# RoPE on one core: 64 rows of x to a partition, tables spread by TensorE, products from staged x

## The chip, the core and the metric

One of the eight cores of a Trainium2 chip. The metric is the device time of one execution in microseconds (us), lower is better; a kernel's number is the median of several runs, with the lowest and highest behind it. A profile is of one execution and its times count from the start of the profiled span, which is some 1.9 us shorter than the time of that run.

## The reference

```python
# x: (8, 8, 1024, 64) float32; cos_cached, sin_cached: (1024, 32) float32
x_first, x_second = x[..., :32], x[..., 32:]
out_first  = x_first * cos_cached - x_second * sin_cached
out_second = x_first * sin_cached + x_second * cos_cached
out = concatenate([out_first, out_second], axis=-1)
```

Each element of x is multiplied by a sine and by a cosine, and one half row is combined with the other. 16.8 MB come in and 16.8 MB go out. The tables are 128 KB each and are used 64 times over.

## The kernel before

x is cut into 16 chunks of 128 partitions by 32 rows (8 KB to a partition). A partition's 32 rows repeat every 32 partitions, so the tables are loaded once to 32 partitions and copied to the other 96: into PSUM for VectorE's products, into SBUF for GpSimd's. VectorE makes nearly all products; the sums go to GpSimd, to TensorE (with ScalarE copying back) or stay on VectorE.

```python
R = 32; F = R * hd; T = R * half; Q = seq // R; reps = P // Q      # Q = 32, reps = 4
csp = pt.tile([P, T], fp32, name="csp")      # PSUM, 2 banks each
snp = pt.tile([P, T], fp32, name="snp")
acc = pa.tile([P, F], fp32, name="acc")      # PSUM, 4 banks
nc.sync.dma_start(out=sn[0:Q], in_=sin_cached.rearrange("(p n) j -> p (n j)", p=Q))
nc.scalar.dma_start(out=cs[0:Q], in_=cos_cached.rearrange("(p n) j -> p (n j)", p=Q))
# ... all loads of x are issued at once ...
for r in range(reps):
    nc.vector.tensor_copy(out=snp[r * Q:(r + 1) * Q], in_=sn[0:Q])
    nc.scalar.copy(out=csp[r * Q:(r + 1) * Q], in_=cs[0:Q])

def products(eng, c, s, ctab, stab):
    xr = rows(xt[c])
    eng.tensor_tensor(out=rows(s), in0=xr, in1=tab(stab), op=TT.mult)
    eng.tensor_tensor(out=xr, in0=xr, in1=tab(ctab), op=TT.mult)
# ... per chunk: products on VectorE, then sums on GpSimd / TensorE / VectorE, then the store;
#     chunks 1 and 6 are GpSimd's alone, chunk 15 VectorE's alone
```

## Time and profile before

| | before |
|---|---|
| time, median (three runs) | 86.01 us (85.86 to 86.02) |
| span of the profiled run | 84.16 us |
| tables landed (sine, cosine) | 3.81, 4.13 |
| first product on VectorE | 8.87 |
| VectorE idle between first product and its end | 2.80 us in all |
| VectorE's last instruction ends | 77.18 |
| last byte stored | 82.70 |

The page's shares, the slices, the stretches and the end of the timeline stand in the prediction below. VectorE's timeline at the start (start and duration in us, then what it waited for in brackets) shows the table copies, from the landing to the first product, and one short wait for x:

```profile
3.84 5.00 DVE L73 COPY snp<-sn 32x1024 f32<-32x1024 f32 x4 [3.84 <-DMA sn<-in_sin_cached_dram]
8.87 2.29 DVE L88 TENSOR_TENSOR vs<-x,snp 128x2048 f32<-128x2048 f32 x1
...
13.99 2.29 DVE L88 TENSOR_TENSOR vs<-x,snp 128x2048 f32<-128x2048 f32 x1 [0.44 <-DMA x<-in_x_dram]
```

TensorE's timeline of the same kernel: each group is one float32 matmul that the trace shows as two. The second starts 1.83 us after the first, the fourth 0.86 us after the third. I read this as half clock for the first two ("cold") and a clock that was released about 3.5 us after the first began. It is read from the pace alone: the page's row of granted clock has nines at that time.

```profile
13.65 2.04 PE L119 MATMUL acc<-x,plus 128*128 128x512 f32 x2 [13.65 <-DVE x L89]
15.48 1.83 PE L120 MATMUL acc<-vs,minus 128*128 128x512 f32 x2
17.15 1.02 PE L119 MATMUL acc<-x,plus 128*128 128x512 f32 x2
18.01 1.02 PE L120 MATMUL acc<-vs,plus 128*128 128x512 f32 x2
```

### The profile page before, as it was taken

Reading aid. Unit: us, or ns where it says so; the run is one execution under the profiler, and the core shown is the slowest. Engines: PE = TensorE matmul, PEld = TensorE weight load, DVE = VectorE, ACT = ScalarE, POOL = GpSimd, SP = SyncE. Lnnn points to the kernel's source line nnn. Section 1 sums busy time; section 2 is a strip of 40 time slices with the busy share of each in tenths; the row PEclk is TensorE's granted clock in tenths of the full one; section 3 lists DMA queues with packets and bytes.
Section 4 is the critical chain, followed back from the end, with each engine's and each line's share of the span. In section 5 each row is a group of like instructions: output and inputs, shape, how many; then the busy total and the mean of one; then the engine's idle time right before and its main releaser. Section 6 shows DMA issues by size and latency. Waiting matters only on the chain.

```text
span 84.2 us, 363 instructions
## 1 busy us (share of the span) xinstructions
PE 40.1 (48%) x80; PEld 15.7 (19%) x80; DVE 70.4 (84%) x34; ACT 15.7 (19%) x16; POOL 71.4 (85%) x38
## 2 busy tenths in 40 slices
PE   0000005994930896895949497794949600000000
PEld 0000002422400341423314051332414100000000
DVE  0199997999999999999999982999999999996000
ACT  4399000004040003104040402204040310000000
POOL 3199999999999999999999999999999999970000
PEclk9999999999999569999999999999999999555555
DMA  3899999999999999999999999999999999999991
GB/s 29 282 432 409 420 420 436 417 409 420 436 428 409 417 428 432 432 424 409 421 436 436 432 421 417 424 424 436 432 432 432 413 421 428 428 436 407 432 419 55
DMA packets 4736, 33.82 MB, mean 402 GB/s; under 512 B 448, under 2 KB 448, under 8 KB 768
## 3 DMA queue, kind: packets, MB, share of 16 engines
q1 hardware_dynamic: 3824, 27.40, 78.7%
q10 hardware_dynamic: 912, 6.42, 18.1%
HBM read 17.04 MB, written 16.78 MB: 402 GB/s over the span
## 4 chain that ended last, share of the span: by engine, by line
POOL 53%; DVE 23%; issue 9%; DMA 4%; DVEq 1%; POOLq 0%
POOL x L94 13%; POOL x L93 11%; DVE vs L88 11%; POOL x L89 11%; POOL gs L88 11%; DVE x L89 8%; POOL sn L77 4%; DMA sn<-in_sin_cached_dram 4%; POOL cs L77 3%; DVE acc L88 3%; DVE x L93 1%; DVEq L170 1%; POOLq L93 0%; POOLq L77 0%
## 5 line engine op out<-in xcount | busy, mean ns | idle before, releaser
L119 PE MATMUL acc<-x,plus 128*128 128x512 f32 x40 | 23.3, 666 | 26.4 <-DVE x L89 13.6
L89 DVE TENSOR_TENSOR x<-x,csp 128x2048 f32<-128x2048 f32 x14 | 32.0, 2287 | 0.6
L88 DVE TENSOR_TENSOR vs<-x,snp 128x2048 f32<-128x2048 f32 x13 | 29.7, 2282 | 2.2 <-POOL x L94 1.7
L122 ACT COPY x<-acc 128x1024 f32<-128x1024 f32 x10 | 10.1, 1012 | 49.2 <-PE acc L120 49.2
L94 POOL TENSOR_TENSOR x<-x,vs 128x1024 f32<-128x1024 f32 (+1 forms) x9 | 19.0, 2108 | 0.0
L93 POOL TENSOR_TENSOR x<-x,vs 128x1024 f32<-128x1024 f32 (+1 forms) x9 | 18.9, 2105 | 0.0
L119 PEld LDWEIGHTS acc<-x,plus 128*128 128x128 f32 x40 | 7.5, 208 | 39.4 <-issue 23.9
L120 PE MATMUL acc<-vs,minus 128*128 128x512 f32 x20 | 11.6, 666 | 0.0
L120 PE MATMUL acc<-vs,plus 128*128 128x512 f32 x20 | 10.2, 592 | 0.0
L89 POOL TENSOR_TENSOR x<-x,cs 128x2048 f32<-128x2048 f32 x2 | 9.1, 4546 | 0.2
L88 POOL TENSOR_TENSOR gs<-x,sn 128x2048 f32<-128x2048 f32 x2 | 9.1, 4542 | 0.1
L73 DVE COPY snp<-sn 32x1024 f32<-32x1024 f32 x4 | 4.9, 1223 | 3.9 <-DMA sn<-in_sin_cached_dram 3.8
L120 PEld LDWEIGHTS acc<-vs,minus 128*128 128x128 f32 x20 | 4.4, 219 | 5.9 <-issue 5.9
L77 POOL COPY sn<-sn 32x1024 f32<-32x1024 f32 x3 | 3.1, 1032 | 2.7 <-DMA sn<-in_sin_cached_dram 2.6
L93 POOL TENSOR_TENSOR x<-x,gs 128x1024 f32<-128x1024 f32 x2 | 4.7, 2362 | 0.2
L94 POOL TENSOR_TENSOR x<-x,gs 128x1024 f32<-128x1024 f32 x2 | 4.7, 2357 | 0.0
L120 PEld LDWEIGHTS acc<-vs,plus 128*128 128x128 f32 x20 | 3.8, 190 | 4.8 <-issue 4.8
L74 ACT COPY csp<-cs 32x1024 f32<-32x1024 f32 x4 | 4.0, 1008 | 1.5 <-DMA cs<-in_cos_cached_dram 1.4
L77 POOL COPY cs<-cs 32x1024 f32<-32x1024 f32 x3 | 3.1, 1033 | 0.1
L88 DVE TENSOR_TENSOR acc<-x,snp 128x2048 f32<-128x2048 f32 x1 | 2.3, 2297 | 0.0
L71 ACT ACT_TABLE_LOAD x1 | 1.3, 1283 | 1.2 <-PEq L159 1.2
L93 DVE TENSOR_TENSOR x<-x,acc 128x1024 f32<-128x1024 f32 x1 | 1.2, 1223 | 0.0
(8 smaller groups left out, 2.4 us busy)
## 6 DMA issues: line engine op xcount, KB each, us to landing
x<-in_x_dram SPq DMA_DIRECT2D x7, 2048.0 KB, 25.0
out_dram<-x SPq DMA_DIRECT2D x9, 1024.0 KB, 13.0
out_dram<-x ACTq DMA_DIRECT2D x6, 1024.0 KB, 9.0
x<-in_x_dram SPq DMA_DIRECT2D x2, 1024.0 KB, 6.3
out_dram<-x SPq DMA_DIRECT2D x2, 512.0 KB, 6.0
cs<-in_cos_cached_dram ACTq DMA_DIRECT2D x1, 128.0 KB, 3.4
sn<-in_sin_cached_dram SPq DMA_DIRECT2D x1, 128.0 KB, 3.1
```

What stands on the lines that cost most here:

```text
L71: nc.scalar.mul(minus, plus, -1.0)
L73: nc.vector.tensor_copy(out=snp[r * Q:(r + 1) * Q], in_=sn[0:Q])
L74: nc.scalar.copy(out=csp[r * Q:(r + 1) * Q], in_=cs[0:Q])
L77: nc.gpsimd.tensor_copy(out=t[r * Q:(r + 1) * Q], in_=t[0:Q])
L88: eng.tensor_tensor(out=rows(s), in0=xr, in1=tab(stab), op=TT.mult)
L89: eng.tensor_tensor(out=xr, in0=xr, in1=tab(ctab), op=TT.mult)
L93: eng.tensor_tensor(out=xr[:, :, 0], in0=xr[:, :, 0], in1=sr[:, :, 1], op=TT.subtract)
L94: eng.tensor_tensor(out=xr[:, :, 1], in0=xr[:, :, 1], in1=sr[:, :, 0], op=TT.add)
L119: nc.tensor.matmul(a[:, k], plus, xr[:, :, k], start=True, stop=False)
L120: nc.tensor.matmul(a[:, k], plus if k else minus, sr[:, :, 1 - k], start=False, stop=True)
L122: nc.scalar.copy(out=xr, in_=a.rearrange("p k n j -> p n k j"))
L170: with _tile.TileContext(nc) as tc:
```

## The change

It means to cut the number of DMA packets (DMA is busy from end to end) by giving a partition 64 rows, so 16 KB packets instead of 8 KB. With 64 rows the tables repeat every 16 partitions and are twice as large, and would take all the eight banks of PSUM that the kernel before divides between tables and sums; so they live in SBUF. Three things follow. TensorE spreads them from 16 partitions to 128 with a matrix of zeros and ones. The first unit's products read the tables from PSUM, where TensorE has put them, while ScalarE copies them to SBUF. From then on ScalarE copies ("stages") each chunk of x to PSUM, and VectorE multiplies the staged chunk by the SBUF table.

```diff
-    R = 32
+    R = 64
-    csp = pt.tile([P, T], fp32, name="csp")
-    snp = pt.tile([P, T], fp32, name="snp")
-    acc = pa.tile([P, F], fp32, name="acc")
+    st = [ps.tile([P, 3 * BK], fp32, name=f"st{i}") for i in range(2)]   # PSUM, 3 banks each
+    acc = ps.tile([P, 2 * BK], fp32, name="acc")                         # PSUM, 2 banks
...
-    for r in range(reps):                       # copies of the tables
-        nc.vector.tensor_copy(out=snp[r * Q:(r + 1) * Q], in_=sn[0:Q])
-        nc.scalar.copy(out=csp[r * Q:(r + 1) * Q], in_=cs[0:Q])
+    part_s = [st[0][:, 0:BK], st[0][:, BK:2 * BK], st[0][:, 2 * BK:], acc[:, :BK]]
+    part_c = [st[1][:, 0:BK], st[1][:, BK:2 * BK], st[1][:, 2 * BK:], acc[:, BK:]]
+    for i in range(4):
+        for t, part in ((sn, part_s), (cs, part_c)):
+            nc.tensor.matmul(part[i], sel, t[0:Q, i * BK:(i + 1) * BK], start=True, stop=True)
...
+    def stage(u, i, n0, n1):
+        nc.scalar.copy(out=st[i][:, :(n1 - n0) * hd], in_=xt[u][:, n0 * hd:n1 * hd])
+    def products(u, i, n0, n1, alone):
+        ...
+        mul(nc.vector, sr, pr, tab(sn, n0, n1))
+        mul(nc.vector, pr if alone else xr, pr, tab(cs, n0, n1))
...
+    for i in range(4):                          # unit 0, straight from the tables in PSUM
+        direct(i)
+        pool_sums(0, i * G, (i + 1) * G)
+    for t, part in ((sn, st[0]), (cs, st[1])):
+        nc.scalar.copy(out=t[:, 0:2 * BK], in_=part[:, 0:2 * BK])
+    ...                                         # and the four remaining parts, 512 each
...
+    cuts = ((0, 24), (24, 48), (48, 64))        # three chunks to a unit of 64 rows
+    ahead = {1: [(pe_back, 1, 0)], 7: [(pe_back, 3, 16)], 10: [(pe_back, 4, 16)]}
+    behind = { ... }                            # sums, copies back and stores, chunk by chunk
+    put(0); put(1)                              # put = stage the chunk
+    for c, (u, n0, n1) in enumerate(chunks):
+        products(u, c % 2, n0, n1, (u, n0) in alone)
+        for f, *args in ahead.get(c, ()): f(*args)
+        put(c + 2)
+        for f, *args in behind.get(c, ()): f(*args)
```

More of the change, by code (lines that the diff above doesn't have):

```diff
@@ L28 @@
     Q = seq // R
-    reps = P // Q
-    n_ch = (b * h * seq) // (R * P)
-    G = 512 // half
-    assert seq % R == 0 and P % Q == 0 and Q % 32 == 0
+    n_u = (b * h * seq) // (R * P)
+    BK = 512
+    G = BK // half
+    assert seq % R == 0 and P % Q == 0 and n_u == 8 and R == 4 * G
     xf = x.rearrange("b h s d -> (b h s d)").rearrange(
-        "(c p m) -> c p m", p=P, m=F)
+        "(u p m) -> u p m", p=P, m=F)
     of = out.rearrange("b h s d -> (b h s d)").rearrange(
-        "(c p m) -> c p m", p=P, m=F)
+        "(u p m) -> u p m", p=P, m=F)
     ctx.enter_context(tc.manual_schedule())
@@ L41 @@
     xp = ctx.enter_context(tc.tile_pool(name="xp", bufs=1))
-    tv = ctx.enter_context(tc.tile_pool(name="tv", bufs=6))
+    tv = ctx.enter_context(tc.tile_pool(name="tv", bufs=3))
     tg = ctx.enter_context(tc.tile_pool(name="tg", bufs=1))
-    pt = ctx.enter_context(
-        tc.tile_pool(name="pt", bufs=1, space=bass.MemoryType.PSUM))
-    pa = ctx.enter_context(
-        tc.tile_pool(name="pa", bufs=1, space=bass.MemoryType.PSUM))
+    ps = ctx.enter_context(
+        tc.tile_pool(name="ps", bufs=1, space=bass.MemoryType.PSUM))
     cs = const.tile([P, T], fp32, name="cs")
     sn = const.tile([P, T], fp32, name="sn")
+    sel = const.tile([Q, P], fp32, name="sel")
     plus = const.tile([P, P], fp32, name="plus")
     minus = const.tile([P, P], fp32, name="minus")
-    csp = pt.tile([P, T], fp32, name="csp")
-    snp = pt.tile([P, T], fp32, name="snp")
-    acc = pa.tile([P, F], fp32, name="acc")
-    nc.sync.dma_start(out=sn[0:Q], in_=sin_cached.rearrange("(p n) j -> p (n j)", p=Q))
-    nc.scalar.dma_start(out=cs[0:Q], in_=cos_cached.rearrange("(p n) j -> p (n j)", p=Q))
-    xt = []
-    for first, n in [(0, 1), (1, 1)] + [(c, 2) for c in range(2, n_ch, 2)]:
-        t = xp.tile([P, n, F], fp32, name=f"x{first}")
-        nc.sync.dma_start(out=t, in_=xf[first:first + n].rearrange("c p m -> p c m"))
-        xt += [t[:, i] for i in range(n)]
+    st = [ps.tile([P, 3 * BK], fp32, name=f"st{i}") for i in range(2)]
+    acc = ps.tile([P, 2 * BK], fp32, name="acc")
+    nc.sync.dma_start(out=sn[0:Q], in_=sin_cached.rearrange("(q n) j -> q (n j)", q=Q))
+    nc.scalar.dma_start(out=cs[0:Q], in_=cos_cached.rearrange("(q n) j -> q (n j)", q=Q))
+    xt = [xp.tile([P, F], fp32, name=f"x{u}") for u in range(n_u)]
+    for m0, m1 in ((0, F // 2), (F // 2, F)):
+        nc.sync.dma_start(out=xt[0][:, m0:m1], in_=xf[0][:, m0:m1])
+    for u in range(1, n_u):
+        nc.sync.dma_start(out=xt[u], in_=xf[u])
+    nc.gpsimd.memset(sel, 0.0)
+    s3 = sel.rearrange("q (r j) -> q r j", j=Q)
+    nc.gpsimd.affine_select(out=s3, in_=s3, compare_op=TT.not_equal, fill=1.0,
+                            base=0, pattern=[[0, P // Q], [-1, Q]], channel_multiplier=1)
     nc.gpsimd.memset(plus, 0.0)
@@ L71 @@
     nc.scalar.mul(minus, plus, -1.0)
-    for r in range(reps):
-        nc.vector.tensor_copy(out=snp[r * Q:(r + 1) * Q], in_=sn[0:Q])
-        nc.scalar.copy(out=csp[r * Q:(r + 1) * Q], in_=cs[0:Q])
-    for t in (sn, cs):
-        for r in range(1, reps):
-            nc.gpsimd.tensor_copy(out=t[r * Q:(r + 1) * Q], in_=t[0:Q])
-    def rows(t, n0=0, n1=R):
+    part_s = [st[0][:, 0:BK], st[0][:, BK:2 * BK], st[0][:, 2 * BK:], acc[:, :BK]]
+    part_c = [st[1][:, 0:BK], st[1][:, BK:2 * BK], st[1][:, 2 * BK:], acc[:, BK:]]
@@ L80, in rows, with tab @@
+    for i in range(4):
+        for t, part in ((sn, part_s), (cs, part_c)):
+            nc.tensor.matmul(part[i], sel, t[0:Q, i * BK:(i + 1) * BK], start=True, stop=True)
+    def rows(t, n0, n1):
         return t[:, n0 * hd:n1 * hd].rearrange("p (n k j) -> p n k j", k=2, j=half)
-    def tab(t, n0=0, n1=R):
+    def tab(t, n0, n1):
         v = t[:, n0 * half:n1 * half].rearrange("p (n o j) -> p n o j", o=1, j=half)
         return v.to_broadcast([P, n1 - n0, 2, half])
-    def products(eng, c, s, ctab, stab):
-        xr = rows(xt[c])
-        eng.tensor_tensor(out=rows(s), in0=xr, in1=tab(stab), op=TT.mult)
-        eng.tensor_tensor(out=xr, in0=xr, in1=tab(ctab), op=TT.mult)
@@ L91, in sums @@
-    def sums(eng, c, s, n0, n1):
-        xr, sr = rows(xt[c], n0, n1), rows(s, n0, n1)
-        eng.tensor_tensor(out=xr[:, :, 0], in0=xr[:, :, 0], in1=sr[:, :, 1], op=TT.subtract)
-        eng.tensor_tensor(out=xr[:, :, 1], in0=xr[:, :, 1], in1=sr[:, :, 0], op=TT.add)
-    def store(q, c, n0=0, n1=R):
-        q.dma_start(out=of[c][:, n0 * hd:n1 * hd], in_=xt[c][:, n0 * hd:n1 * hd])
-    def on_pool(c):
-        s = tg.tile([P, F], fp32, name="gs")
-        products(nc.gpsimd, c, s, cs, sn)
-        sums(nc.gpsimd, c, s, 0, R)
-        store(nc.sync, c)
@@ L105, in vector_pool @@
-    def vector_pool(c, cuts=(0, R)):
-        s = tv.tile([P, F], fp32, name="vs")
-        products(nc.vector, c, s, csp, snp)
-        for n0, n1 in zip(cuts, cuts[1:]):
-            sums(nc.gpsimd, c, s, n0, n1)
-            store(nc.sync, c, n0, n1)
-    def vector_tensor(c):
-        s = tv.tile([P, F], fp32, name="vs")
-        products(nc.vector, c, s, csp, snp)
-        for n0 in range(0, R, G):
-            xr, sr = rows(xt[c], n0, n0 + G), rows(s, n0, n0 + G)
-            a = acc[:, n0 * hd:(n0 + G) * hd].rearrange("p (k n j) -> p k n j", k=2, j=half)
-            for k in range(2):
-                nc.tensor.matmul(a[:, k], plus, xr[:, :, k], start=True, stop=False)
-                nc.tensor.matmul(a[:, k], plus if k else minus, sr[:, :, 1 - k],
-                                 start=False, stop=True)
-            nc.scalar.copy(out=xr, in_=a.rearrange("p k n j -> p n k j"))
-        store(nc.scalar, c)
@@ L125, in vector_alone, with mul @@
-    def vector_alone(c):
-        products(nc.vector, c, acc, csp, snp)
-        sums(nc.vector, c, acc, 0, R)
-        store(nc.scalar, c)
-    vector_tensor(0)
-    on_pool(1)
-    vector_pool(2)
-    vector_pool(3)
-    vector_tensor(4)
-    on_pool(6)
-    vector_pool(5)
-    vector_tensor(7)
-    vector_pool(8)
-    vector_tensor(9)
-    vector_pool(10)
-    vector_tensor(11)
-    vector_pool(12)
-    vector_pool(13)
-    vector_pool(14, (0, G, R))
-    vector_alone(15)
+    def mul(eng, o, a, t):
+        eng.tensor_tensor(out=o, in0=a, in1=t, op=TT.mult)
@@ new lines, in sums, with direct @@
+    def sums(eng, o, c, s):
+        eng.tensor_tensor(out=o[:, :, 0], in0=c[:, :, 0], in1=s[:, :, 1], op=TT.subtract)
+        eng.tensor_tensor(out=o[:, :, 1], in0=c[:, :, 1], in1=s[:, :, 0], op=TT.add)
+    sv = {}
+    def direct(i):
+        if 0 not in sv:
+            sv[0] = tv.tile([P, F], fp32, name="s")
+        n0, n1 = i * G, (i + 1) * G
+        xr = rows(xt[0], n0, n1)
+        mul(nc.vector, rows(sv[0], n0, n1), xr, tab(part_s[i], 0, G))
+        mul(nc.vector, xr, xr, tab(part_c[i], 0, G))
@@ new lines, in stage, with on_pool @@
+    def stage(u, i, n0, n1):
+        nc.scalar.copy(out=st[i][:, :(n1 - n0) * hd], in_=xt[u][:, n0 * hd:n1 * hd])
+    def products(u, i, n0, n1, alone):
+        if u not in sv:
+            sv[u] = tv.tile([P, F], fp32, name="s")
+        xr, sr, pr = rows(xt[u], n0, n1), rows(sv[u], n0, n1), rows(st[i], 0, n1 - n0)
+        mul(nc.vector, sr, pr, tab(sn, n0, n1))
+        mul(nc.vector, pr if alone else xr, pr, tab(cs, n0, n1))
+        if alone:
+            sums(nc.vector, xr, pr, sr)
+    def on_pool(u, n0, n1):
+        g = tg.tile([P, F // 2], fp32, name="g")
+        xr, gr = rows(xt[u], n0, n1), rows(g, 0, n1 - n0)
+        mul(nc.gpsimd, gr, xr, tab(sn, n0, n1))
+        mul(nc.gpsimd, xr, xr, tab(cs, n0, n1))
+        sums(nc.gpsimd, xr, xr, gr)
@@ new lines, in pool_sums, with pe_sums @@
+    def pool_sums(u, n0, n1):
+        xr = rows(xt[u], n0, n1)
+        sums(nc.gpsimd, xr, xr, rows(sv[u], n0, n1))
+    a = acc.rearrange("p (k n j) -> p k n j", k=2, j=half)
+    def pe_sums(u, n0):
+        xr, sr = rows(xt[u], n0, n0 + G), rows(sv[u], n0, n0 + G)
+        for k in range(2):
+            nc.tensor.matmul(a[:, k], plus, xr[:, :, k], start=True, stop=False)
+            nc.tensor.matmul(a[:, k], plus if k else minus, sr[:, :, 1 - k],
+                             start=False, stop=True)
@@ new lines, in pe_back, with store @@
+    def pe_back(u, n0):
+        nc.scalar.copy(out=rows(xt[u], n0, n0 + G), in_=a.rearrange("p k n j -> p n k j"))
+    def store(q, u, n0=0, n1=R):
+        q.dma_start(out=of[u][:, n0 * hd:n1 * hd], in_=xt[u][:, n0 * hd:n1 * hd])
+    for i in range(4):
[3 more added lines that the diff above has]
+        nc.scalar.copy(out=t[:, 0:2 * BK], in_=part[:, 0:2 * BK])
+    for i in (2, 3):
+        for t, part in ((sn, part_s), (cs, part_c)):
+            nc.scalar.copy(out=t[:, i * BK:(i + 1) * BK], in_=part[i])
@@ new lines @@
+    on_pool(2, 0, 32)
+    on_pool(2, 32, 64)
+    store(nc.sync, 2)
+    cuts = ((0, 24), (24, 48), (48, 64))
+    chunks = [(u, n0, n1) for u in (1, 3, 4, 5, 6, 7) for n0, n1 in cuts]
+    alone = {(1, 48), (7, 24), (7, 48)}
+    ahead = {1: [(pe_back, 1, 0)], 7: [(pe_back, 3, 16)], 10: [(pe_back, 4, 16)]}
+    behind = {
+        0: [(store, nc.scalar, 0), (pe_sums, 1, 0)],
+        1: [(pe_sums, 1, 16)],
+        2: [(pe_back, 1, 16), (pe_sums, 1, 32)],
+        3: [(pe_back, 1, 32), (pe_sums, 3, 0)],
+        4: [(store, nc.scalar, 1)],
+        5: [(pe_back, 3, 0), (pe_sums, 3, 16), (pool_sums, 3, 32, 64)],
+        7: [(store, nc.sync, 3), (pe_sums, 4, 0)],
+        8: [(pe_back, 4, 0), (pe_sums, 4, 16), (pool_sums, 4, 32, 64)],
+        10: [(store, nc.sync, 4), (pe_sums, 5, 0)],
+        11: [(pe_back, 5, 0), (pool_sums, 5, 16, 64), (store, nc.sync, 5)],
+        12: [(pe_sums, 6, 0)],
+        13: [(pe_back, 6, 0), (pool_sums, 6, 16, 48)],
+        14: [(pool_sums, 6, 48, 64), (store, nc.sync, 6)],
+        15: [(pool_sums, 7, 0, 24)],
+        16: [(store, nc.sync, 7, 0, 48)],
+        17: [(store, nc.scalar, 7, 48, 64)],
+    }
@@ L148, with put @@
+    def put(c):
+        if c < len(chunks):
+            u, n0, n1 = chunks[c]
+            stage(u, c % 2, n0, n1)
+    put(0)
+    put(1)
+    for c, (u, n0, n1) in enumerate(chunks):
+        products(u, c % 2, n0, n1, (u, n0) in alone)
+        for f, *args in ahead.get(c, ()):
+            f(*args)
+        put(c + 2)
+        for f, *args in behind.get(c, ()):
+            f(*args)
 _INS = ['x', 'cos_cached', 'sin_cached']
```

## The prediction

> **What bounds the kernel now.** I read the page's shares first, then the slices, then the stretches with DMA shares, then the timeline of the end, and last the DMA packet records of the trace.
>
> ```profile
> PE 40.1 (48%) x80; PEld 15.7 (19%) x80; DVE 70.4 (84%) x34; ACT 15.7 (19%) x16; POOL 71.4 (85%) x38
> ...
> DMA  3899999999999999999999999999999999999991
> GB/s 29 282 432 409 420 420 436 417 409 420 436 428 409 417 428 432 432 424 409 421 436 436 432 421 417 424 424 436 432 432 432 413 421 428 428 436 407 432 419 55
> ...
> q1 hardware_dynamic: 3824, 27.40, 78.7%
> q10 hardware_dynamic: 912, 6.42, 18.1%
> ```
>
> No engine is full (84 and 85% at most), but the 16 DMA engines are: their row is 9 from the third slice to the last but one, and the two queues' packets together take 96.8% of 16 engines' span.
>
> ```profile
> 40.00:60.00 20.00, 15.59 (x35) 6.10 (x34) 18.12 (x9) 4.05 (x4) 19.92 (x9) 1.00 1.01 427
> 60.00:77.00 17.00, 5.42 (x13) 1.85 (x11) 16.83 (x9) 2.02 (x2) 15.27 (x9) 0.84 1.01 426
> 77.00:80.00 3.00, 0.00 (x0) 0.00 (x0) 0.19 (x1) 0.00 (x0) 0.00 (x0) 0.50 1.05 430
> 80.00:82.00 2.00, 0.00 (x0) 0.00 (x0) 0.00 (x0) 0.00 (x0) 0.00 (x0) 0.50 0.96 408
> ```
>
> The last two numbers are the DMA share and GB/s. DMA is full after all arithmetic has ended.
>
> ```profile
> 72.51 2.29 DVE L89 TENSOR_TENSOR x<-x,csp 128x2048 f32<-128x2048 f32 x1
> ...
> 75.97 1.21 DVE L94 TENSOR_TENSOR x<-x,acc 128x1024 f32<-128x1024 f32 x1
> ```
>
> Arithmetic ends at 77.18 us, the span at 84.16. The last store is 1 MB, some 2.5 us of transfer at 424 GB/s; DMA was busy 5.5 us after it was issued. So about 3 us of older stores still stood in the queues: the arithmetic runs 3 us ahead of the transfers. The chain of waits goes back through GpSimd and VectorE, but it is read from the last instruction, not from the last byte. Bound by DMA with 3 us to spare: that is the reading.
>
> **What the Trainium skill says.** "DMA: Bandwidth & Descriptors", section "Where 436 GB/s comes from", puts the ports' ceiling at 435 GB/s; the best slices here have 436. Its section "Why small descriptors are slow (HBM only)" names a fixed cost per packet. The records agree that there is one: the median 8 KB packet took 309 ns and the median 4 KB one 159 ns, so 4 KB cost 150 ns and each packet 9 ns.
> "TensorE: Matmul & The Clock Gate", Part 1, says the array starts at half clock and is let go after about 3.4 us of activity, in windows that do not start with the kernel. Here the first matmul starts at 13.65 and the second follows 1.83 us later; from 17.15 on they follow at 0.86 us. It agrees.
> "PSUM — Partial Sum Buffer", section "PSUM bank collisions raise a hardware error", asks that engines be kept apart by bank. The built program of the changed kernel does it with waits, and coarsely; they decide my prediction.
> "SBUF — State Buffer", section "Who interferes with whom": VectorE with two SBUF inputs contends with GpSimd. Both kernels keep one input of each VectorE product in PSUM (first the tables, now x); before, those took 2282 to 2287 ns with GpSimd busy beside them. I expect no contention after either.
>
> **The change part by part.**
>
> *Descriptors.* x moves 33.55 MB, 2.10 MB per DMA engine. Before, an engine has 248 packets of 8 KB, 20 of 4 KB and 28 for semaphores: 296. After: 14 whole transfers with 8 packets of 16 KB each, 32 smaller ones (the halved first load, the 48 and 16 rows of the last store), 2 for the tables, 20 for semaphores: 166. The 130 saved at 9 ns are 1.2 us. By the same fit a 16 KB packet takes 609 ns. This alone would make 86.0 into 84.8.
>
> *VectorE.* 2048 elements start every 4.52 / 2 = 2.26 us (starts at 18.52, 23.04, 27.56 for two), that is 1.042 ns an element and 0.127 us each. A unit of 64 rows was four instructions and 9.04 us; it is now six (2 x 1536, 1536, 1024) without waits on itself between products, some 9.0 us: nothing gained. Sums done by VectorE alone grow from 2048 elements to 3584, +1.6 us. Its table copies (5 us, to 8.87) go.
>
> *The start, which replaces them.* The first product waits in the built program until the fifth table matmul has ended (all three of one PSUM tile), not the first. Tables landed at 3.81 and 4.13; on 16 partitions instead of 32 I take 4.2. The first three matmuls run cold at about 1.75, two warm at 0.86: 7.0 us. First product at 11.2, against 8.87 before; 10.3 if two are cold, 12.1 if four. The eight direct products of 1024 (1.19 each) take 9.6: to 20.8.
>
> *The handover.* The staging tiles are the table tiles. ScalarE may copy the tables out only behind VectorE's reads of the same tile, so the last half-bank copy follows the eighth product. From the 1024-element copy's 1.01 us I estimate 0.58 us for 512 elements and 1.43 us for the 1536-element staging (1024 elements from SBUF to PSUM took 1.008). 20.9 + 0.58 + 1.43 = 22.9: VectorE, after 2.2 us idle, goes on at 23.0.
>
> *Steady state.* ScalarE has some 38 us of work in all, so it is no bound, but its queue is in order and a staging copy sometimes stands behind a copy out of TensorE's sums. Laying the queues side by side with these durations I get two stalls of about 0.5 us. Unit 1 has 1.3 us of sums alone. Units 1, 3, 4, 5 end at 23.0 + 4 x 9.0 + 1.3 + 0.5 = 60.8.
>
> *GpSimd and the stores.* A unit's sums are now one late, large piece. Unit 2 alone takes GpSimd 2 x 13.8 us, to some 51 (4.53 for each product, 2.28 to 2.36 for each sum). The sums of 48 rows of unit 5 can start only at 60.8: 2 x 3.35 (estimated from 2.28 per 1024, 1.21 per 512) gives 67.5, and its store goes out at 67.6. Unit 6: chunk two is ready at 61.3 + 6.9 = 68.2, then 2 x 2.29 and 2 x 1.21, so its store goes out at 75.3. What is then still to move is 8 x 609 ns, 8 x 459 (48 rows) and 8 x 159 (16 rows): 9.8 us. With 1.0 from issue to first packet (0.73 to 1.77 before), 75.3 + 1.0 + 9.8 = 86.1. From last packet to the span's end was 84.16 - 82.70 = 1.46, and the time is 86.01 - 84.16 = 1.85 above the span: 86.1 + 1.46 + 1.85 = **89.4 us**.
> Check from the side of DMA: starting at 1.8, with 0.9 lost at the start as now, loads take about 39.6 and five stores 24.4, so DMA is dry at 66.7 and waits for unit 5 (first packet 68.6) some 1.9 us; that one ends at 73.5 and unit 6 starts at 76.3, 2.8 us more. About 4.7 us of idle DMA against 1.2 us saved: +3.5.
> VectorE ends at 61.3 + 2 x 9.0 + 3.2 = 82.5; its last store of 0.5 MB would end near 84.9, before the 86.1 above.
>
> **The rivals.**
> *DMA stays the bound (84.8 us).* For it: DMA is full today and the packets get cheaper. Against: the 3 us of slack must carry a start 2.3 us later, a 2.2 us handover, 1.6 us more sums and coarser stores. It needs the start and the handover to be much shorter than I read.
> *TensorE stays cold longer, or 16 table rows don't wake it.* A window more at half clock puts the first product at 12.1, and all that follows moves with it: 90.3, with all eight cold about 91. For it: the windows are not tied to the kernel. Against: full activity in the trace warmed it in 3.5 us.
> *ScalarE's order stalls VectorE each chunk.* If every third staging copy came 0.5 us late, 3 us: 92. The 1.01 us copies and the TensorE group's 3.79 us say that there is room most of the time.
> *The tables' load.* Sixteen partitions may take the load more slowly; 0.5 us would go straight into the start: 89.9.
>
> **Range and chances.** The spread of the first product (10.3 to 12.1) is +-0.9, the stalls +1 to -1, the descriptor gain +-0.5, errors of the laid-out queues +-1. I predict 89.4 us, 87.2 to 91.6 in 8 of 10. Slower by over 2% (87.7) 0.81; within 2% 0.14; faster 0.05.
>
> **What would show it.** Right: the first product near 11 us just behind the fifth table matmul; VectorE idle some 2 us around 21 to 23 until a ScalarE copy; DMA slices below 9 between about 66 and 77; packets of 16 KB at 609 ns; the unit 6 store issued near 75; the last byte after 85. Wrong: DMA slices of 9 throughout (then 84.8 holds and the slack was larger), a first product before 9, or 16 KB packets off the 609 ns line.

## The result, and the profile after

The kernel after takes 96.35 us (95.76 to 96.76, four runs), the kernel before beside it 86.02 (85.86 to 86.39). Executions over 1.5% slower than the fastest of the same kernel are left out of the means. Ratios here are the mean time of one kernel's fast runs over that of the other's in the same rounds, so not quite the ratio of the medians: 1.1189, with a 95% interval of 1.112 to 1.1259. It is slower, as predicted, but by 10.3 us where 3.4 were predicted, and outside the range.

The page of the kernel after. The busy line, then VectorE's and the DMA's slices in tenths, then the two queues:

```profile
PE 49.0 (52%) x88; PEld 18.8 (20%) x88; DVE 67.9 (72%) x50; ACT 37.2 (40%) x35; POOL 65.1 (69%) x36
...
DVE  0000007999359998699979997999799999999600
...
DMA  0999999989999989999999729997695297099992
...
q1 hardware_dynamic: 2192, 28.97, 73.9%
q10 hardware_dynamic: 464, 4.85, 12.7%
```

Where the kernel before had a row of nines, DMA now has holes from the 23rd slice on. VectorE starts in the seventh slice and no engine is near full. The packets' time is as long as before (86.6% of 93.8 us is 81.2, and 96.8% of 84.2 was 81.5), so all of the extra time is time in which DMA had nothing to move.

VectorE's timeline, cut to the instructions that waited, the last direct product and the last instruction:

```profile
14.21 1.22 DVE L90 TENSOR_TENSOR s<-x,st 128x1024 f32<-128x1024 f32 x1 [14.21 <-PE st L80]
15.92 1.22 DVE L90 TENSOR_TENSOR x<-x,st 128x1024 f32<-128x1024 f32 x1 [0.49 <-PE st L80]
...
23.07 1.22 DVE L90 TENSOR_TENSOR x<-x,acc 128x1024 f32<-128x1024 f32 x1
26.84 1.76 DVE L90 TENSOR_TENSOR s<-st,sn 128x1536 f32<-128x1536 f32 x1 [2.54 <-ACT st L108]
...
38.41 1.76 DVE L90 TENSOR_TENSOR s<-st,sn 128x1536 f32<-128x1536 f32 x1 [1.23 <-ACT st L108]
...
87.74 0.68 DVE L94 TENSOR_TENSOR x<-st,s 128x512 f32<-128x512 f32 x1
```

The first product is 5.3 us later than before. Three further stalls, at 48.09 (0.66 us), 57.62 (0.53) and 67.29 (0.65), are left out here. TensorE's timeline says why the start is so late:

```profile
5.30 2.04 PE L80 MATMUL st<-sn,sel 16*128 16x512 f32 x2 [5.30 <-DMA sn<-in_sin_cached_dram]
7.14 1.91 PE L80 MATMUL st<-cs,sel 16*128 16x512 f32 x2
...
12.26 1.91 PE L80 MATMUL st<-sn,sel 16*128 16x512 f32 x2
...
17.38 1.91 PE L80 MATMUL acc<-cs,sel 16*128 16x512 f32 x2
30.52 2.04 PE L136 MATMUL acc<-x,plus 128*128 128x512 f32 x2 [11.22 <-DVE x L90]
...
34.06 1.07 PE L136 MATMUL acc<-x,plus 128*128 128x512 f32 x2
```

From the second on, the eight table matmuls follow each other at 1.71 us, from 5.30 to 19.29: 14.0 us of unbroken work that contracts 16 rows, all at the cold pace. The 128-row matmuls from 30.52 on are at 0.9 us within 3.6 us, much as in the kernel before. The page's row of granted clock shows neither cold stretch (it has nines at both); the pace of the matmuls does. The first product waits for the fifth matmul (12.26 + 1.91 = 14.17).

ScalarE's timeline around the first stall of the staged part: its copy back (L141) waits 4.66 us for TensorE, still cold, and the staging copies for VectorE's next chunks (L108) stand behind it in the same queue.

```profile
30.35 1.02 ACT L108 COPY st<-x 128x1024 f32<-128x1024 f32 x1 [2.17 <-DVE x L90]
...
36.02 1.01 ACT L141 COPY x<-acc 128x1024 f32<-128x1024 f32 x1 [4.66 <-PE acc L137]
36.93 2.82 ACT L108 COPY st<-x 128x1536 f32<-128x1536 f32 x2
```

And the stretches near the end, of which the last two numbers are DMA share and GB/s: two holes, each ended by a store that was issued late (units 5 and 6, at 73.64 and 81.28). A third, of 2.2 us, is at 53.6 to 55.7.

```profile
72.00:74.50 2.50, 2.48 (x6) 0.76 (x4) 2.50 (x3) 0.38 (x1) 1.94 (x2) 1.00 0.11 46
74.50:79.00 4.50, 0.00 (x0) 0.00 (x0) 4.50 (x4) 3.35 (x3) 4.50 (x3) 0.95 1.04 441
79.00:82.00 3.00, 0.00 (x0) 0.00 (x0) 3.00 (x3) 1.02 (x1) 3.00 (x3) 0.50 0.00 0
```

From VectorE's end (77.18 before, 88.42 after: 11.24 later) the books can be closed. The first product is 5.34 later, VectorE is busy 2.38 more from there on (67.90 against 65.52, the last without the table copies), and it idles 3.50 more (6.30 against 2.80). Together 11.22. The tail from there to the end of the span is 1.57 shorter (5.40 against 6.97): from the last store's issue to the last byte it is 3.7 us (88.45 to 92.19) where it was 5.5 (77.22 to 82.70). Most of that is the size of the last store, 0.5 MB in place of 1 MB: 8 packets of 159 ns to an engine instead of 8 of 309, so 1.2 us less. That leaves the 9.65 by which the spans differ.

### The profile page after: what moved, and what is told of

Same layout as the page of the kernel before. It is cut to its first block, busy times and chain, and to the rows that moved or that the text cites. A ratio compares the mean times of both kernels' runs of the same rounds, so it can differ in the third digit from the quotient of the medians.

```text
span 93.8 us, 424 instructions
## 1 busy us (share of the span) xinstructions
PE 49.0 (52%) x88; PEld 18.8 (20%) x88; DVE 67.9 (72%) x50; ACT 37.2 (40%) x35; POOL 65.1 (69%) x36
## 5 line engine op out<-in xcount | busy, mean ns | idle before, releaser
L90 DVE TENSOR_TENSOR s<-st,sn 128x1536 f32<-128x1536 f32 (+1 forms) x18 | 28.3, 1572 | 5.6 <-ACT st L108 5.0
L93 POOL TENSOR_TENSOR x<-x,s 128x512 f32<-128x512 f32 (+3 forms) x10 | 18.6, 1858 | 18.6 <-DVE x L90 15.4
L108 ACT COPY st<-x 128x1536 f32<-128x1536 f32 (+1 forms) x18 | 23.1, 1305 | 6.8 <-DVE x L90 6.5
L90 DVE TENSOR_TENSOR x<-st,cs 128x1536 f32<-128x1536 f32 (+1 forms) x15 | 24.1, 1605 | 0.0
L94 POOL TENSOR_TENSOR x<-x,s 128x512 f32<-128x512 f32 (+3 forms) x10 | 18.6, 1860 | 0.0
L141 ACT COPY x<-acc 128x1024 f32<-128x1024 f32 x9 | 9.1, 1012 | 16.9 <-PE acc L137 16.9
L137 PE MATMUL acc<-s,minus 128*128 128x512 f32 x18 | 10.1, 644 | 0.0
L137 PE MATMUL acc<-s,plus 128*128 128x512 f32 x18 | 9.2, 592 | 0.0
L90 POOL TENSOR_TENSOR g<-x,sn 128x2048 f32<-128x2048 f32 x2 | 9.1, 4529 | 0.1
L80 PE MATMUL st<-sn,sel 16*128 16x512 f32 x6 | 5.9, 1078 | 5.3 <-DMA sn<-in_sin_cached_dram 5.3
L80 PE MATMUL st<-cs,sel 16*128 16x512 f32 x6 | 5.7, 1056 | 0.0
L93 POOL TENSOR_TENSOR x<-x,g 128x1024 f32<-128x1024 f32 x2 | 4.7, 2357 | 0.2
L94 POOL TENSOR_TENSOR x<-x,g 128x1024 f32<-128x1024 f32 x2 | 4.7, 2368 | 0.0
```

The costliest lines, as they stand in the source:

```text
L80: nc.tensor.matmul(part[i], sel, t[0:Q, i * BK:(i + 1) * BK], start=True, stop=True)
L90: eng.tensor_tensor(out=o, in0=a, in1=t, op=TT.mult)
L93: eng.tensor_tensor(out=o[:, :, 0], in0=c[:, :, 0], in1=s[:, :, 1], op=TT.subtract)
L94: eng.tensor_tensor(out=o[:, :, 1], in0=c[:, :, 1], in1=s[:, :, 0], op=TT.add)
L108: nc.scalar.copy(out=st[i][:, :(n1 - n0) * hd], in_=xt[u][:, n0 * hd:n1 * hd])
L137: nc.tensor.matmul(a[:, k], plus if k else minus, sr[:, :, 1 - k], start=False, stop=True)
```

## The experiments

Theory: DMA is no longer the bound, because everything after waits on VectorE, and VectorE is late for three separate reasons: the tables (late landing, cold matmuls), the coarse wait of a product on a whole PSUM tile, and the order in ScalarE's queue. Rivals: the late start is hidden by the slack and the coarser stores are what costs; or the 16 KB packets themselves are slow. The first four experiments ran on one chip beside the kernel before (85.99 us), the next four beside it at 85.95, the last two at 85.97. All gave the reference's result. The kernel after was not run again beside them; the kernel before, which differs by 0.1 us between the sessions, ties them to its 96.35 us. The readings of stalls and landings come from one profiled run each, and two things vary in those with no edit behind it: when the sine table lands (4.26 to 5.37 us in the four runs that load it to 16 partitions) and how soon a cold TensorE picks up its pace (below).

### Tables over 128 partitions

The tables go to 128 partitions in rows of 1 KB, and sixteen matmuls of 256 columns spread them, contracting 128 rows: as many columns streamed as before, in the same order.

```diff
-    nc.sync.dma_start(out=sn[0:Q], in_=sin_cached.rearrange("(q n) j -> q (n j)", q=Q))
+    nc.sync.dma_start(out=raw_s, in_=sin_cached.rearrange("(q n) j -> q (n j)", q=P))
...
-            nc.tensor.matmul(part[i], sel, t[0:Q, i * BK:(i + 1) * BK], start=True, stop=True)
+            for h in range(2):
+                nc.tensor.matmul(part[i][:, h * BK // 2:(h + 1) * BK // 2], sel[:, 2 * i + h], t,
+                                 start=True, stop=True)
```

> The changed kernel with the tables loaded over 128 partitions and spread by matmuls that contract 128 rows instead of 16 (sixteen of 256 columns, the same columns in all). Theory: the array's clock is let go by activity and 16 of 128 rows don't count; then the clock rises some 3.5 to 6.8 us into the table matmuls here, the first VectorE product comes at 10 to 12 us instead of 14.2, and as VectorE's chain sets the end, the time falls by as much: 92.5 to 94.5 us. Rival: the clock stays low in the first 14 us whatever the rows; then only the tables' earlier landing counts, about 1 us: 95 to 95.7 us.

92.92 us (92.75 to 93.17), ratio 1.0806 (1.0769 to 1.0842): 3.4 us less than the kernel after. TensorE's timeline of this run, where a group is now half as many columns times twice as many matmuls:

```profile
3.47 2.05 PE L82 MATMUL st<-raw_s,sel 128*128 128x256 f32 x4 [3.47 <-DMA raw_s<-in_sin_cached_dram]
...
7.02 1.34 PE L82 MATMUL st<-raw_s,sel 128*128 128x256 f32 x4
8.20 1.03 PE L82 MATMUL st<-raw_c,sel 128*128 128x256 f32 x4
```

The tables land at 3.33 and 3.50 instead of 5.17 and 5.35, and the time for 512 columns falls to 0.86 us after 4.2 us of work. The first product starts at 10.12, 4.1 us earlier than after; a part of that is given back in the stall at the fourth staged chunk (2.16 instead of 1.23). TensorE went cold again between the tables and the first sums, here for longer: the copy back starts 6.43 us after the first of these sums (26.05 to 32.48), in the kernel after 5.50 (30.52 to 36.02). The difference, 0.93, is that of the stalls. Nothing in the edit asks for it.

### A PSUM tile for each table part

```diff
-    part_s = [st[0][:, 0:BK], st[0][:, BK:2 * BK], st[0][:, 2 * BK:], acc[:, :BK]]
-    part_c = [st[1][:, 0:BK], st[1][:, BK:2 * BK], st[1][:, 2 * BK:], acc[:, BK:]]
+    part_s = ps_[0:3] + ps_[6:7]          # eight tiles of one bank each, in a pool that is
+    part_c = ps_[3:6] + ps_[7:8]          # released before the staging tiles are made
```

> The changed kernel with one PSUM tile for each of the eight table parts, so that a product waits for its own part and not for the whole tile. Theory (the wait for five matmuls is what makes VectorE late): first product at about 7.8 us (bound by x landing), the eighth ends at about 20.5 us, paced by cold matmuls of 1.71 us, the first staged product starts at about 22.5 instead of 26.8, and the time falls by about 4: 91.5 to 92.8 us. Rival (the start is hidden, and GpSimd's late sums set the stores): under 1 us of change.

91.63 us (90.66 to 92.54); two of the four runs count as slow, and the ratio of the two fast ones (90.66 and 91.18, mean 90.92) is 1.057 (1.0511 to 1.0629), so some 5.4 us less than the kernel after. The profiled run is one of the slow ones (92.54), so its times may run late. VectorE's start in it:

```profile
7.76 1.22 DVE L89 TENSOR_TENSOR s<-x,t 128x1024 f32<-128x1024 f32 x1 [7.76 <-DMA x<-in_x_dram]
...
10.99 1.22 DVE L89 TENSOR_TENSOR s<-x,t 128x1024 f32<-128x1024 f32 x1 [0.49 <-PE t L79]
...
22.87 1.76 DVE L89 TENSOR_TENSOR s<-st,sn 128x1536 f32<-128x1536 f32 x1 [2.13 <-ACT st L107]
```

The first product no longer waits for five matmuls but for x, and from then on each product waits some 0.49 us for the next cold matmul, at 1.71 us a step. The staged part starts at 22.87 instead of 26.84. So the wait in the built program, for all matmuls into one three-bank tile, cost about 4 us here, on top of the cold pace. (0.4 of it is the shorter handover, 2.13 for 2.54; the edit also copies the tables out in eight parts instead of six.)

### Staging ahead of the copies back

Four copies back move behind the staging copy that they stood ahead of in ScalarE's queue.

```diff
-    ahead = {1: [(pe_back, 1, 0)], 7: [(pe_back, 3, 16)], 10: [(pe_back, 4, 16)]}
+    ahead = {}
-        1: [(pe_sums, 1, 16)],
+        1: [(pe_back, 1, 0), (pe_sums, 1, 16)],
...                                        # likewise at chunks 3/4, 7 and 10
```

> The changed kernel with four copies back from TensorE's sums moved behind the staging copy that stood behind them in ScalarE's queue; nothing else. Theory: VectorE's four idle stretches in the staged part (1.23, 0.66, 0.53 and 0.65 us) are made by that order; they go, and the time falls by 2.4 to 3.1 us: 93.3 to 94 us. Rival (they are made by late TensorE sums or by something else): they move and the time stays within 1 us of 96.3.

93.16 us (92.69 to 93.5), ratio 1.0828 (1.078 to 1.0876): 3.2 us less. The stalls behind the handover fall from 3.07 us in four to 1.64 in three (0.45, 0.59, 0.60). That is less than the time gained. Against the profiled run of the kernel after (span 93.82 to 90.74, so 3.08) the rest is 0.91 from a sine table that landed earlier in this run (4.26 for 5.17), which the edit did not cause, 0.1 of VectorE's busy time, and 0.64 in the tail behind VectorE's end, whose cause I don't know. About 1.4 us are the edit's by the trace, half of the 2.4 to 3.1 that I expected.

### The kernel before, started late

Does a late start alone explain it? In the kernel before, VectorE copies something useless five times ahead of its first product.

```diff
+    for _ in range(5):
+        nc.vector.tensor_copy(out=acc[:, 0:1024], in_=csp[:, 0:1024])
     vector_tensor(0)
     on_pool(1)
```

> The kernel before with five idle PSUM copies on VectorE ahead of its first product, so that it starts near 15 us as in the changed kernel instead of 8.9 (some 6 us late). My reading of 3 us of slack under DMA says that half of it is hidden: 88.5 to 90 us. If there is no slack, 92; if DMA hides it all, 86.

87.51 us (87.18 to 87.7), ratio 1.0163 (1.0119 to 1.0208). The first product is at 15.13, 6.26 later and even later than in the kernel after (14.21), and yet the time grows by 1.5 us only (1.2 to 2.1%), less than I expected (88.5 to 90). The page's rows of VectorE and DMA:

```profile
DVE  0199999999999999999999999999999999999600
...
DMA  1999999999999999999999999999999989998591
```

VectorE's waits shrink from 2.80 us to 0.52, so its end moves by 3.67 only (77.18 to 80.86); of these another 2.2 vanish in the queue of older stores. By this estimate the slack of the kernel before was about 4.7 us (6.26 - 1.5), not the 3 that I read from its last store: some 2.2 us lay between arithmetic and DMA, and 2.3 more in VectorE's own waits. So a late start alone is not why the kernel after is slow. There VectorE has 2.4 us more work, and the start's delay doesn't eat other waits but comes with new ones.

### All three edits together

The three diffs of the first three experiments, applied to one kernel.

> The three mends together in the changed kernel: tables over 128 partitions with 128-row matmuls, a PSUM tile for each table part, staging ahead of the copies back. If VectorE's chain is the bound and the three causes are separate, the first product comes at about 6.5 us (x landing), the first staged one at about 18.5, VectorE ends near 78 instead of 88.4, DMA is full again almost to the end, and the time is 84.8 to 86.0 us, at or a little below the kernel before. If something else than these three holds the changed kernel back (16 KB packets, GpSimd's late sums), it stays above 88.

86.58 us (86.01 to 86.98, six runs), ratio 1.005 (0.9999 to 1.0101): 9.8 us less than the kernel after, and within the noise of the kernel before, but above the 84.8 to 86.0 that I expected. One by one the edits gained 3.4, 5.4 (fast runs) and 3.2, in all 12.0. The rows of VectorE and DMA on its page, and then the line of VectorE's timeline at the handover:

```profile
DVE  3108999729999999999999999999979999997000
...
DMA  1999999999998999999999999999999999999960
```

```profile
18.55 1.76 DVE L92 TENSOR_TENSOR s<-st,sn 128x1536 f32<-128x1536 f32 x1 [2.13 <-ACT st L110]
```

The holes in the DMA row are gone, and the last byte is at 83.10. The first product is at 6.51, VectorE ends at 77.64, 10.8 us earlier than after. So DMA looks like the bound again (the last experiment tests it), and the sum of the three single gains isn't reached. That the edits overlap (the first two both shorten the wait for cold matmuls) can be a part of it.

### The same with 8 KB packets

Each 16 KB transfer in two halves, nothing else changed against the last one.

```diff
-        nc.sync.dma_start(out=xt[u], in_=xf[u])
+        for m0, m1 in ((0, F // 2), (F // 2, F)):
+            nc.sync.dma_start(out=xt[u][:, m0:m1], in_=xf[u][:, m0:m1])
...                                        # stores likewise, 32 rows at a time
```

> The same, with every transfer of x cut into two of 8 KB a partition (32 rows), stores too. Where DMA is the bound, the 9 us-thousandths that each packet costs over its bytes should show: 16 packets more per engine and direction for each pair, some 1.0 to 1.2 us in all, so 1 us slower than the run beside it. If VectorE's chain still binds, or finer stores help more than packets cost, no difference or a little faster.

86.46 us (86.36 to 86.75), ratio 1.0056 (1.0026 to 1.0086). No difference to the 16 KB version, where I had expected about 1 us. The packets' records do show the gain per byte: the median 8 KB packet takes 309 ns and the median 16 KB one 611, so 7 ns are saved in 618. All packets' time over 16 engines is 81.44 us here and 80.54 with 16 KB. But the ends are equal. In the 16 KB run, DMA shows a slow spell at 24 to 27 us (311 GB/s), soon after its first store, and in the last 0.8 us packets come one at a time, as from one engine that finished after the others; the slow spell is in this 8 KB run too (339 GB/s). The profiled spans average 84.3 us with 16 KB and 84.5 with 8 KB; the time outside of the span is 2.2 and 2.0 us. Where the rest of the 0.9 us went is open.

### Tables over 32 partitions

To split the first experiment into its two halves: tables as the kernel before loads them (32 partitions, 4 KB rows), and matmuls that contract 32 rows.

```diff
-    nc.sync.dma_start(out=sn[0:Q], in_=sin_cached.rearrange("(q n) j -> q (n j)", q=Q))
+    nc.sync.dma_start(out=sn[0:2 * Q, 0:T // 2], in_=sin_cached.rearrange("(q n) j -> q (n j)", q=2 * Q))
...
-            nc.tensor.matmul(part[i], sel, t[0:Q, i * BK:(i + 1) * BK], start=True, stop=True)
+            nc.tensor.matmul(part[i], sel[:, i // 2], t[0:2 * Q, (i % 2) * BK:(i % 2 + 1) * BK], start=True, stop=True)
```

> The changed kernel with the tables on 32 partitions (4 KB rows) and matmuls that contract 32 rows. Two questions. Landing: if it is the 16 partitions that made the tables land at 5.2 us, they land near 3.8 to 4.2 as in the kernel before. Clock: if the array counts rows in use, 32 rows either let the clock go by 8 us or don't; with 16 they did not in 13.9 us of matmuls, with 128 they did in 4.2 us. I lean to no, as 32 rows are a quarter.

One look, a single run whose state is unknown: 94.28 us (the kernel after's profiled run had 95.76). TensorE's first and last table matmul:

```profile
3.96 2.04 PE L81 MATMUL st<-sn,sel 32*128 32x512 f32 x2 [3.96 <-DMA sn<-in_sin_cached_dram]
...
16.04 1.91 PE L81 MATMUL acc<-cs,sel 32*128 32x512 f32 x2
```

The tables land at 3.83 and 4.20, so it was the load to 16 partitions (or its 8 KB rows) that made them late. Over all runs the sine table landed at 4.26 to 5.37 us on 16 partitions (four runs), 3.81 to 3.87 on 32 (three) and 3.31 to 3.35 on 128 (five). The load to 16 also holds up what comes behind it: most of the first packets of x took 1.0 to 1.2 us in the kernel after, where those of the kernel before took at most 0.62, and the first piece of x landed at 7.60 us, against 6.48 before and 6.40 with tables over 128 partitions. But the pace stays at 1.71 us to the end: 32 rows don't bring the fast pace either. The first product is at 12.87, 1.34 earlier than after, and the single time is 1.5 us shorter. So of the first experiment's 4.1 us at the first product, some 1.8 are the landing (5.30 to 3.47 at TensorE) and 2.3 the pace.

With 128 rows, every cold stretch of matmuls in the twelve runs reached the fast pace, but not after a fixed time: in the kernel before the third matmul from 27.74 on is fast, 3.3 us later (31.02). In the 8 KB version above, the first four are slow and only the fifth is fast, 7.8 us after the first, with a pause of 1.1 us before it:

```profile
22.14 2.05 PE L138 MATMUL acc<-x,plus 128*128 128x512 f32 x2 [9.42 <-DVE x L93]
...
29.92 1.12 PE L138 MATMUL acc<-x,plus 128*128 128x512 f32 x2 [1.10 <-ACT x L144]
```

The 16- and 32-row matmuls stayed slow for 14.0 us, in four runs and in one. What isn't shown is that it is the clock: a matmul of few rows could run at this pace whatever the clock is. In no run does one follow warm 128-row matmuls closely, and the row of granted clock, with its nines, can't decide it.

### The kernel after with 8 KB packets

The diff of the 8 KB version above, on the kernel after itself.

> The changed kernel with every transfer of x cut into two of 8 KB a partition and nothing else. Theory (DMA waits for stores there, its packets are not the bound): within 1 us of 96.3, rather faster, as each half of a unit can be stored when its sums are done. Rival (16 KB packets are what is slow): 91 us or less.

95.38 us (94.69 to 95.62), ratio 1.1076 (1.1022 to 1.113): 1 us less than with 16 KB. VectorE ends at 88.58 in it, 0.16 later than after. The last byte is at 91.11 all the same, 1.1 us earlier. The packets' size is not what slows the kernel after; that halves of a unit can be stored sooner is my reading of the 1 us, and not split off.

### Staging beside the last direct products

One wait of size was left in the combined version, the 2.13 us of the handover. Here the sums' tile has its own pool, so that the first staging copy no longer waits for the last table part.

```diff
-    ps_ = [tb.tile([P, BK], fp32, name=f"t{i}") for i in range(8)]
+    acc = pa.tile([P, 2 * BK], fp32, name="acc")                      # its own pool
+    ps_ = [tb.tile([P, BK], fp32, name=f"t{i}") for i in range(6)]
+    ps_ += [acc[:, 0:BK], acc[:, BK:]]
...
     put(0)
+    for t, part in ((sn, part_s), (cs, part_c)):
+        nc.scalar.copy(out=t[:, 3 * BK:4 * BK], in_=part[3])
     put(1)
```

> The combined version (tables over 128 partitions, a PSUM tile for each table part, staging ahead of the copies back) once more, but the sums' PSUM tile now has its own pool, so that the first staging copy no longer waits for the last table part: it can run beside the last direct products. Theory, the handover's idle was the last VectorE wait of any size but DMA is already the bound: VectorE's idle ahead of the first staged product falls from 2.1 to about 0.3 us and VectorE ends near 75.5 to 76, but DMA slices stay at 9 and the time is 85.0 to 86.2, at most 1 us below the combined version beside it. Rival, VectorE's end still sets the time: 84.5, the whole 2 us. If time falls under 84.3 (2% below the kernel before), both are wrong.

> The combined version again, to stand beside the one with the early staging on the same chip. All theories: 86.0 to 87.0, idle of 2.1 us ahead of the first staged product; the difference of the two runs is what counts.

86.92 us (86.73 to 87.18), ratio 1.0112 (1.0089 to 1.0134), and the combined version beside it 86.76 (86.23 to 87.26), ratio 1.0101 (1.0076 to 1.0126). In the run with early staging the handover's idle is gone (the first staged product has no wait in brackets any more):

```profile
16.29 1.75 DVE L96 TENSOR_TENSOR s<-st,sn 128x1536 f32<-128x1536 f32 x1
```

It gained nothing in the time, which is above the 85.0 to 86.2 that I expected. VectorE ends at 76.73 against 77.29 in the run beside it, so only 0.6 us of the 2.1 was gained even there; most of the rest came back as later waits for staging (1.8 us in four, against 0.6 in the run beside it). The DMA rows of both are nines, with a few eights, to the last slice but two. And the last store was issued 0.56 us earlier than in the run beside it (76.76 for 77.32) but landed no earlier (82.89 for 82.82). So DMA, and not VectorE, ends the combined version.

No version here beats the kernel before: both ratios are clear of 1. Most of what is lost lies outside of the profiled span. The spans average 84.2 us (before), 84.4 (combined) and 84.3 (early staging), while the time is 1.8, 2.3 and 2.7 us longer than the span. No run says what the program does there.

## Why the prediction was right and wrong

The direction and the mechanism held: VectorE becomes late, DMA runs dry late in the kernel (its slices have holes from the 23rd on, the widest around 72 to 74 and 79 to 82 us), and the store of unit 6 sets the end. 16 KB packets took 613 ns (609 predicted), the 1536-element staging 1.45 (1.43) and the half-bank copy 0.59 (0.58). VectorE and GpSimd did not slow each other, as expected: 1024-element products took 1.21 us with GpSimd busy (at 54.76) and idle (at 64.29). The size was off by 7 us. Term by term, along the prediction's own sum:

| term | predicted | measured | off by |
|---|---|---|---|
| tables landed, TensorE starts | 4.2 | 5.30 | +1.1 |
| five matmuls | 7.0 | 8.9 | +1.9 |
| direct products | 9.6 | 10.1 | +0.5 |
| handover | 2.2 | 2.54 | +0.3 |
| first staged product to the end of unit 5 | 37.8 | 39.8 | +2.0 |
| unit 5 to the issue of unit 6's store | 14.5 | 14.6 | +0.1 |
| that store to the last byte | 10.8 | 10.9 | +0.1 |
| last byte to the reported time | 3.3 | 4.2 | +0.9 |

The last row compares the profiled run's last byte (92.19) with the median of all four runs, of which the profiled one was the fastest; 0.6 of it is that.

- The step that failed first is "The first three matmuls run cold at about 1.75, two warm at 0.86: 7.0." All eight ran cold. I had seen the fast pace come 3.5 us after the first matmul in the kernel before, and took that for any matmul. The runs show that it depends on the rows contracted: matmuls of 16 and 32 rows did not get there in 14.0 us, those of 128 did in 3.3 to 7.8, in all twelve runs. (That the clock stayed low is the likely reading; see the tables over 32 partitions.) I had the right rival on the list ("TensorE stays cold longer, or 16 table rows don't wake it") and gave its full form 91 us and too small a chance.
- "On 16 partitions instead of 32 I take 4.2" was wrong by 1 us. The 32- and 128-partition versions landed 1.2 to 1.9 us earlier. "SBUF — State Buffer" of the Trainium skill, section "Door 1: The DMA port swizzle", says that bandwidth depends on how many of the 16 ports the partitions reach, and lists 4 ports for 16 partitions against 8 for 32; the order of the three landings (5.17, 3.83, 3.33 for the sine table) agrees with it. I named this rival too and sized it at 0.5.
- "I get two stalls of about 0.5 us" was the other failing step: four stalls, 3.07 us in all, of which 2.42 came before unit 5's end. They were of the kind I described (a staging copy behind a copy back), but I laid the queues out with warm sums. The first stall was long because TensorE was cold again at 30.52. My rival "ScalarE's order stalls VectorE each chunk", sized at 3 us, is what came: each stall is at the first chunk of a unit. The prediction weighed its rivals one at a time, and three came true together.
- The slack of "3 us" in the kernel before was too small, as the late start shows (4.7). It changes nothing in the sum, which followed VectorE's path directly, but it means that my rival "DMA stays the bound" deserved better reasoning: the combined version, with first product at 6.51 and an unchanged amount of arithmetic, is bound by DMA.
- "1.2 us saved" by descriptors: the records show 0.9 over 16 engines, and no run shows any of it in the time.
- "With 1.0 from issue to first packet" held for stores into an idle DMA (0.83 us for units 5 and 6), but not where the queues were full: the last store waited 2.3 us, the first 3.5.
- "1.042 ns an element and 0.127 us each" does not follow from the one interval given. The kernel after starts products and sums every 1.67, 1.13 and 0.61 us for 1536, 1024 and 512 elements, which makes about 1.04 ns and 0.08 us. The sum hardly changes.

What stays open: whether few-row matmuls are slow by the clock or by themselves; the 0.9 us that the larger packets save and the time doesn't show, with the 0.2 to 0.9 us that the repaired versions take outside of the profiled span; the slow spell of DMA after the first store in the versions that start early; and the 0.64 us in the tail of the run with reordered staging.

## What to carry to other kernels

A change that saves on the bound engine pays only if the work that feeds it stays ahead; here three small delays upstream (tables, a tile-wide wait, a queue's order) cost 10 us, and with all three repaired the saving of 1% never showed: the repaired versions take 0.5 to 1.0 us more than the kernel before. Before putting a setup step on TensorE, look at how many rows it contracts and which tile its result shares, since consumers may wait for the tile's last writer. And measure the slack by delaying the kernel on purpose: it costs one run, and reading it off the last store missed a third of it.

## What the Trainium skill lacked or had wrong

- "TensorE: Matmul & The Clock Gate", Part 1, ties the release to about 3.4 us of activity and does not speak of the rows contracted. Eight float32 matmuls of 16 rows, and eight of 32 rows, back to back for 14.0 us, never reached the fast pace (1.71 us each throughout, whether by the clock or not); 128-row matmuls did after 3.3 us (before, from 27.74), 3.6 (after, from 30.52), 4.2 (tables over 128 partitions) and up to 7.8 (8 KB version, from 22.14).
- "DMA: Bandwidth & Descriptors" gives about 0.6 us to the first byte on the hardware path, without saying from where it counts. The four stores of the kernel after that were issued into an idle DMA took 0.83 to 0.85 us to their first packet from the start of the issuing instruction, which itself takes 0.33, so this doesn't contradict it. What it lacks is the wait behind full queues: 2.3 us (last store of the kernel after), 3.5 (its first) and 4.1 (the first of the combined version).
- The same page gives a cost per packet of about 3 cycles in one place and about 10.5 ns, for small packets, in another; here it is 9 ns (4 and 8 KB). What it lacks is what large packets are still worth: going from 8 to 16 KB saves 7 ns in 618, and two versions that differ in this alone took 86.58 and 86.46 us.
- "PSUM — Partial Sum Buffer" sets its rule by bank and quadrant. The waits in the built program go by tile, which is the software's doing and not the chip's: a product that reads one bank waited for the matmuls into all three banks of the tile, which cost 4 us (first staged product 26.84 against 22.87 with one tile for each bank). The page doesn't have it.
- "SBUF — State Buffer", Door 1, lists bandwidth for large transfers alone. For a 128 KB table that runs ahead of the loads of x, 16, 32 and 128 partitions landed at 5.17, 3.83 and 3.33 us.
